# The first two feature tiles multiplied in parts of 256 tokens, with 256 columns normed first

## The chip, the cores and the metric

The kernel runs on one core of a Trainium2 chip. Its time is that of one execution on the device in microseconds (us); the figure for a kernel is the median of several executions. The engines are TensorE (PE in the profile, with PEld for its weight loads), ScalarE (ACT), VectorE (DVE), GpSimd (POOL) and SyncE (SP), which issues most DMAs.

## What is computed

One layer of a diffusion backbone over 1024 tokens of width 1024, with 256 context tokens. The part that matters here is the beginning: the adaLN modulation of the normed input, and the first column products with `w_in`.

```python
shift, scale, gate = adaln(c, w_ada, b_ada)          # silu(c) @ w_ada + b_ada
h = rmsnorm(x, norm_g) * (1 + scale[:, None]) + shift[:, None]
q, k, v, za, u, bg, cg, zc = jnp.split(h @ w_in, SPLIT_POINTS, axis=-1)
...
attn = neighbourhood_attention(q, k, heads(v), kc, vc, rpb) * jax.nn.silu(za)
conv = bg * centred_short_conv(cg * u, conv_w, conv_b) * jax.nn.silu(zc)
x_new = x + gate[:, None] * (jnp.concatenate([attn, conv], axis=-1) @ w_out)
```

## The kernel before

**Tiles.** The tokens come as eight tiles `xx[0]` to `xx[7]` of 128 tokens by 1024 features, four for each half of the sequence. Each is squared and summed on ACT (`square`, 607), its sum is turned into 1/rms by an addition on DVE and a power on POOL (`root`, 613), and DVE multiplies the tile by it in place (`norm`, 617). PE then transposes 128 features (one of eight feature tiles k) of four token tiles into one PSUM bank, a `tr` tile (`transposed`, 694). There are two buffers of `tr`; the modulation rows `mods[m]` (638) take one of them while they are summed. `turn` (700) applies scale and shift and splits the result into a high part `hh[k]` (ACT, type fp32r) and a low part `hl[k]`: a second copy in full precision, `hw`, is made by ACT or DVE, and DVE subtracts the high part from it (`modulated`, 673).

**Products.** `first_columns(half, k)` (719) multiplies three blocks of 128 columns of `w_in` (for u, the gate and c) by the 512 tokens of one half: high by high, low weights by high, high weights by low, nine matmuls into three PSUM banks `acc0`, which collect over all eight k. The weights come as chunks (`load_chunks`, 563); `split_chunk` (764) casts one on ACT and subtracts on DVE. `keep_clock` (586) issues matmuls on zeros that only keep TensorE busy.

**Modulation.** `w_ada` comes in slabs of 256 columns, two for each pair m of feature tiles (shift and scale, `load_slab`, 553). `products(m, j)` (638) multiplies the SiLU of the conditioning by slab (m, j): unsplit for (0, 0), (0, 1) and (1, 0); slab (1, 1) and later ones are split by `cast_slab` (620) and `rest_of` (628) into a high and a low part, with one pass for each. `row_copy` (649) takes the sums to SBUF on ACT (on DVE for m = 0), and `modulation` (655) transposes them and makes scale and shift `ab` on DVE for two feature tiles. So k = 2 and 3 can be turned only when slabs (1, 0) and (1, 1) have gone through.

**What sets the order.** In this section, `strict` (545) holds all engines and SP: every instruction of an engine is chained behind the one written before it (`ordered`, 44 to 60). The order of lines 767 to 834 is thus the order in which each engine works. SP issues loads in the written order (567 to 577, then at 812, 813, 818, 825, 826 and 832). Slabs after the first two share three buffers, so a later load waits until an earlier slab has been read.

Before, all four token tiles of the first half are normed whole and transposed for k = 0 and 1, both are turned and multiplied at 512 tokens, the second half is normed, and then come products(1, 0), the transposes of the second half, the split slab's products(1, 1), and only then `first_columns(1, 0)` (821).

Of the kernel before, what the change touches and what calls it, by code (L numbers as in the profile page):

```python
# [10 lines left out]
F32 = mybir.dt.float32  # L11
F32R = mybir.dt.float32r
BF16 = mybir.dt.bfloat16
AF = mybir.ActivationFunctionType
# [5 lines left out]
P = 128  # L20
# [19 lines left out]
def body(tc, es, x, ctxt, w_ada, b_ada, w_in, q_g, k_g, rpbr, w_out, vecs, cst, out):  # L40
# [522 lines left out]
    def load_chunks(ks):  # L563
        for k in ks:
            chunks[k] = chunk_load(CU, k)

    load_slab(0, 0)
    load_slab(0, 1)
    load_x(range(4))
    load_chunks([0])  # L570
    load_x([4, 5])
    load_chunks([1])
    load_x([6, 7])
    load_slab(1, 0)
    load_slab(1, 1)
# [31 lines left out]
    def square(xtile, n):  # L607

        sqj = cvp.tile([P, D], BF16, name="sqj", tag="cu", bufs=1)
        sums[n] = xp.tile([P, 1], F32, name="xss", tag="xss", bufs=4)  # L610
        act.activation(sqj, xtile, AF.Square, scale=1.0 / 32, accum_out=sums[n])

    def root(n):
        dve.tensor_scalar(sums[n], sums[n], EPS, None, ALU.add)
        pool.tensor_tensor(sums[n], sums[n], mhalf[:, 0:1], ALU.pow)

    def norm(xtile, n):
        dve.tensor_scalar(xtile, xtile, sums[n], None, ALU.mult)

    def cast_slab(m, j, part, cast):  # L620

# [33 lines left out]
    def modulation(m, rw):  # L655

        n, ks = 4 if m else 2, slice(2 * m, 2 * m + 2)
        pm = mods[m]
        for j in range(2):
            for i in range(2):  # L660
                pe.transpose(pm[:, n * (2 * j + i):n * (2 * j + i + 1)], rw[:, 256 * j + i * P:256 * j + (i + 1) * P],
                             ident[:n, :n])
        both = lambda v: v[:, ks].rearrange("p (k o) -> p k o", o=1).broadcast_to([P, 2, 2])
        abk = ab[:, ks].rearrange("p k (w j) -> p j k w", w=2)
        pm = pm[:, 0:4 * n].rearrange("p (j k w) -> p j k w", j=2, k=2)
        dve.tensor_tensor(abk[:, 0], pm[:, 0, :, 0:2], both(bsh), ALU.add)
        dve.tensor_tensor(abk[:, 1], pm[:, 1, :, 0:2], both(b1), ALU.add)
        if n > 2:
            for j in range(2):
                dve.tensor_tensor(abk[:, j], abk[:, j], pm[:, j, :, 2:4], ALU.add)  # L670
        dve.tensor_tensor(abk[:, 1], abk[:, 1], both(ng), ALU.mult)

    def modulated(hi, lo, ps, k, w, on, between=None):

        n = len(ps.shape) > 2 and 512 or 256
# [3 lines left out]
        if n == 512:  # L679
            hv = hv.rearrange("p (r b c) -> p r b c", r=8, b=4)  # L680
        act.activation(hi, ps, AF.Identity, bias=sh, scale=sc)
        if on is act:
            act.activation(hv, ps, AF.Identity, bias=sh, scale=sc)
        else:
            dve.tensor_scalar(hv, ps, sc, sh, ALU.mult, ALU.add)
        if between:
            between()
        dve.tensor_tensor(lo, hv, hi.bitcast(F32), ALU.subtract)

    def rows_of(v, half):  # L690

        return v.rearrange("p (b r c) -> p r b c", b=4, r=16)[:, 8 * half:8 * half + 8]
# [4 lines left out]
        for i in ts:  # L697
            pe.transpose(pts[half, k][:, i * P:(i + 1) * P], xx[4 * half + i][:, k * P:(k + 1) * P], ident)

    def turn(half, k, on, between=None):  # L700

        modulated(rows_of(hh[k], half), rows_of(hl[k], half),
                  pts.pop((half, k))[:].rearrange("p (r b c) -> p r b c", r=8, b=4), k, 0, on, between)

    def transposed_ctx(k2):
        pts[k2] = tr()
# [9 lines left out]
            k = 2 * k2 + kk  # L716
            modulated(hc[k // 4][:, k % 4, 0], hc[k // 4][:, k % 4, 1], pts[k2][:, kk * 256:(kk + 1) * 256], k, 1, (act, dve)[kk])

    def first_columns(half, k, part=range(3)):

        wh, wl = chunks[k][:2]
        h_, l_ = (v.rearrange("p (b r c) -> p b (r c)", b=4, r=16)[:, :, 128 * half:128 * half + 128]
                  for v in (hh[k], hl[k]))
        for i in part:
            for u in (0, 2, 1):
                uc = slice(u * P, (u + 1) * P)
                pe.matmul(acc0[u][half], (wl if i == 1 else wh)[:, uc], l_ if i == 2 else h_,
                          start=k == 0 and i == 0, stop=k == KT - 1 and i == 2)

    def gains_load():  # L730

# [32 lines left out]
    def split_chunk(k):  # L764
        chunks[k] = chunk_split(chunks[k])
# [2 lines left out]

    products(0, 0)
    products(0, 1)  # L770
    square(xx[0], 0)
    root(0)
    keep_clock(2)
    rw = row_copy(0)
    square(xx[1], 1)
    root(1)
    norm(xx[0], 0)
    square(xx[2], 2)
    root(2)
    modulation(0, rw)  # L780
    keep_clock(2)
    for t in range(1, 4):
        for k in range(2):
            transposed(0, k, [t - 1])
        keep_clock((5, 2, 3)[t - 1])
        norm(xx[t], t)
        if t == 1:
            square(xx[3], 3)
            root(3)
    for k in range(2):  # L790
        transposed(0, k, [3])
    split_chunk(0)
    square(xx[4], 4)
    root(4)
    turn(0, 0, dve)
    first_columns(0, 0)
    turn(0, 1, dve, lambda: split_chunk(1))
    for t in range(5, 8):
        square(xx[t], t)
        root(t)  # L800
        norm(xx[t - 1], t - 1)
    first_columns(0, 1)
    norm(xx[7], 7)
    cast_slab(1, 1, 0, act.copy)
    cast_slab(1, 1, 1, dve.tensor_copy)
    rest_of(1, 1, 0)
    rest_of(1, 1, 1)
    products(1, 0, range(6))
    transposed(1, 0)
    products(1, 0, range(6, KT))  # L810
    turn(1, 0, act)
    load_slab(2, 1)
    load_chunks([4, 5])
    products(1, 1, parts=(0,))
# [2 lines left out]
    products(1, 1, range(4, KT), (1,))  # L817
    load_slab(3, 0)
    split_chunk(2)
    turn(1, 1, act)  # L820
    first_columns(1, 0)
    rw = row_copy(1)
    split_chunk(3)
    split(2, 0, 0)
    load_slab(3, 1)
    load_chunks([6, 7])
    transposed(0, 2)
    modulation(1, rw)
# [720 lines left out]
```

## Time and profile before

| what | before |
|---|---|
| median of 3 runs | 631.23 us (630.48 to 631.58) |
| the profiled execution | 630.4 us |
| its span, first to last instruction | 628.6 us |
| mean granted TensorE clock | 0.999 |
| HBM traffic | read 89.04 MB, written 39.04 MB |

The times of single instructions below are from that profiled execution and count from the start of its span. A row of the timeline gives start, duration, engine, line, operation, what it writes and reads, shapes, and in brackets the engine's idle time before it with what ended it. Most instructions here have line 55, since the helper of the strict order emits them; they are told apart by the tiles they write. A row with x18 merges 18 instructions of a kind.

### The profile page before, as it was taken

The numbers are of one execution on the slowest core, as the hardware profiler recorded it, in microseconds if no ns is written. First come the engines' busy times: TensorE is split into PE (matmuls) and PEld (weight loads), VectorE is DVE, ScalarE is ACT, GpSimd is POOL, SyncE is SP. The second block draws the span as 40 slices with busy tenths as digits, with TensorE's granted clock in tenths as the row PEclk, the third lists the DMA queues.
The fourth block names the chain that finished last, engine by engine and source line by source line (L and its number), as shares of the span: only waits on it lengthen the run. The fifth ranks groups of instructions, "written<-read, shape, count | busy, mean of one in ns | idle before, by whom it ended". The sixth has DMA issues, their size and how long they took to land.

```text
span 628.6 us, 10005 instructions
## 1 busy us (share of the span) xinstructions
PE 621.7 (99%) x3487; PEld 538.5 (86%) x3488; DVE 433.5 (69%) x889; ACT 326.5 (52%) x712; POOL 77.6 (12%) x102
## 2 busy tenths in 40 slices
PE   8999999999999999999999999999999999999998
PEld 3577899999999999888888888888888888888887
DVE  1887858866866855568897879988998865594111
ACT  3777835524625545346576568566774845450000
POOL 1305014113223221100000000000000002004200
PEclk9999999999999999999999999999999999999999
DMA  8983737967784995885474553775542235963621
GB/s 316 347 282 124 178 111 259 286 204 244 236 293 137 302 320 181 298 264 214 144 238 140 192 172 127 214 254 181 190 136 76 61 93 163 357 226 121 213 102 50
DMA packets 104030, 126.45 MB, mean 201 GB/s; under 512 B 10689, under 2 KB 70553, under 8 KB 102700
## 3 DMA queue, kind: packets, MB, share of 16 engines
q1 hardware_dynamic: 97516, 114.24, 55.3%
q10 hardware_dynamic: 6208, 11.05, 5.6%
q0 software_dynamic: 256, 0.54, 0.3%
q8 instruction: 27, 0.44, 0.3%
q14 instruction: 23, 0.19, 0.1%
HBM read 89.04 MB, written 39.04 MB: 204 GB/s over the span
## 4 chain that ended last, share of the span: by engine, by line
PE 96%; DMA 2%; SPq 1%; ACT 0%; issue 0%; DVE 0%; ACTq 0%
PE pu L55 29%; PE pacc L55 21%; PE po L55 8%; PE acc L55 6%; PE pout L75 5%; PE pout L74 5%; PE pout L76 5%; PE tr L55 4%; PE cacc L55 4%; PE pss L55 3%; PE pc L55 2%; PE pmx L55 2%; DMA xx<-in_x 2%; PE trA L55 1%; PE trB L55 1%; SPq L55 1%
## 5 line engine op out<-in xcount | busy, mean ns | idle before, releaser
L55 PE MATMUL pu<-h,uh 128*128 128x512 f32 x544 | 170.0, 394 | 0.0
L55 PE MATMUL pacc<-w,h 128*128 128x384 f32 x768 | 138.4, 337 | 0.0
L55 PEld LDWEIGHTS pacc<-w,h 128*128 128x128 f32 x768 | 132.7, 188 | 0.2
L55 PEld LDWEIGHTS pu<-h,uh 128*128 128x128 f32 x544 | 97.6, 188 | 16.8 <-ACT zs L55 0.2
L55 PE MATMUL pu<-h,ul 128*128 128x512 f32 x272 | 106.6, 392 | 0.0
L55 PEld LDWEIGHTS pu<-h,ul 128*128 128x128 f32 x272 | 51.1, 188 | 11.2
L55 POOL TENSOR_TENSOR ss<-ss,few 128x4 f32<-128x4 f32 (+1 forms) x40 | 41.9, 1049 | 124.8 <-DVE ss L55 124.8
L75 PE MATMUL pout<-wol,yh 128*128 128x512 f32 (+2 forms) x136 | 51.6, 379 | 0.0
L74 PE MATMUL pout<-woh,yh 128*128 128x512 f32 (+2 forms) x136 | 51.5, 379 | 0.0
L76 PE MATMUL pout<-woh,yl 128*128 128x512 f32 (+2 forms) x136 | 50.8, 379 | 0.0
L55 PE MATMUL acc<-h,w 128*128 128x512 f32 x144 | 38.1, 404 | 0.8 <-ACT h L55 0.8
L55 ACT ACTIVATE sq<-pacc 128x256 f32<-128x256 f32 x32 | 12.4, 388 | 47.5 <-PE pacc L55 43.7
L55 DVE TENSOR_REDUCE rm<-pmx 128x2 f32<-128x256 f32 (+1 forms) x33 | 13.8, 417 | 32.7 <-PE pmx L55 32.6
L55 ACT COPY mg<-pmx 128x256 f32<-128x256 f32 (+1 forms) x33 | 12.1, 366 | 46.4 <-PE pmx L55 42.0
L55 DVE TENSOR_TENSOR mx<-mx,sb 128x372 f32<-128x372 f32 (+2 forms) x64 | 31.9, 498 | 1.9
L55 PE MATMUL po<-phl,v 128*65 128x276 f32 (+2 forms) x192 | 32.0, 269 | 0.0
L55 DVE TENSOR_REDUCE ss<-sq 128x4 f32<-128x260 f32 (+1 forms) x40 | 15.7, 392 | 23.6 <-ACT sq L55 23.6
L55 ACT ACTIVATE qn<-pacc,ss 128x64 f32<-128x64 f32 x128 | 30.2, 333 | 3.0 <-POOL ss L55 3.0
L55 PEld LDWEIGHTS acc<-h,w 128*128 128x128 f32 x144 | 25.5, 188 | 6.5 <-ACT h L55 1.2
L1479 DVE TENSOR_TENSOR ot<-pout,xr 128x512 f32<-128x512 f32 (+2 forms) x9 | 5.7, 632 | 35.4 <-PE pout L76 33.3
L55 ACT COPY sc<-pc 128x512 f32<-128x512 f32 x32 | 18.8, 589 | 21.1 <-PE pc L55 21.0
L74 PEld LDWEIGHTS pout<-woh,yh 128*128 128x128 f32 x136 | 25.6, 188 | 4.7
(159 smaller groups left out, 1194.4 us busy)
## 6 DMA issues: line engine op xcount, KB each, us to landing
uraw<-in_w_in SPq DMA_DIRECT2D x34, 256.0 KB
q_d<-qs SPq DMA_DIRECT2D x32, 256.0 KB
k_s<-k_d SPq DMA_DIRECT2D x8, 1024.0 KB
q_s<-q_d SPq DMA_DIRECT2D x16, 512.0 KB
wr<-in_w_in SPq DMA_DIRECT2D x40, 192.0 KB
slab<-in_w_ada SPq DMA_DIRECT2D x6, 1024.0 KB
v_d<-vs SPq DMA_DIRECT2D x20, 260.0 KB
v<-v_d SPq DMA_DIRECT2D x16, 325.0 KB
```

The lines of the kernel that those rows point to most:

```text
L55: i = emit(*a, **kw)
L74: i = pe.matmul(ps, ah, bh, start=first, stop=False)
L75: pe.matmul(ps, ah, bl, start=False, stop=False)
L76: pe.matmul(ps, al, bh, start=False, stop=last)
L1479: dve.tensor_tensor(ot[:, c], ps[c.start][:, c], xr[:, c], ALU.add)
```

## The change

The first half of the tokens is taken in two parts q of 256 tokens for k = 0 and 1: `turn` and `first_columns` get an argument q. Token tiles are first normed in columns 0 to 255 alone, which is all that k = 0 and 1 need; the other 768 columns follow later by `norm_rest`, on DVE for tiles 0, 1, 2, 6 and 7 and on ACT for tiles 3, 4 and 5. The loads of x and of the chunks change places, `root` and `norm` change places, `first_columns(1, 0)` stands ahead of the split slab's products, and `row_copy(1)` ahead of `turn(1, 1)`. The casts of slab (1, 1) swap engines. The matmuls of `keep_clock` among these lines go from 2 + 2 + 5 + 2 + 3 to 2 + 4.

```diff
-    load_x(range(4))
+    load_x([0, 1])
     load_chunks([0])
+    load_x([2, 3])
+    load_chunks([1])
     load_x([4, 5])
-    load_chunks([1])
     load_x([6, 7])
...
-        sums[n] = xp.tile([P, 1], F32, name="xss", tag="xss", bufs=4)
+        sums[n] = xp.tile([P, 1], F32, name="xss", tag="xss", bufs=8)
...
-    def norm(xtile, n):
-        dve.tensor_scalar(xtile, xtile, sums[n], None, ALU.mult)
+    def norm(xtile, n, cols=slice(0, D)):
+        dve.tensor_scalar(xtile[:, cols], xtile[:, cols], sums[n], None, ALU.mult)
+
+    def norm_rest(t, on):
+
+        v = xx[t][:, 256:]
+        if on is act:
+            act.activation(v, v, AF.Identity, scale=sums[t])
+        else:
+            dve.tensor_scalar(v, v, sums[t], None, ALU.mult)
...
-    def turn(half, k, on, between=None):
+    def turn(half, k, on, between=None, q=None):
 
-        modulated(rows_of(hh[k], half), rows_of(hl[k], half),
-                  pts.pop((half, k))[:].rearrange("p (r b c) -> p r b c", r=8, b=4), k, 0, on, between)
+        rows = slice(0, 8) if q is None else slice(4 * q, 4 * q + 4)
+        ps = pts[half, k] if q == 0 else pts.pop((half, k))
+        modulated(rows_of(hh[k], half)[:, rows], rows_of(hl[k], half)[:, rows],
+                  ps[:].rearrange("p (r b c) -> p r b c", r=8, b=4)[:, rows], k, 0, on, between)
...
-    def first_columns(half, k, part=range(3)):
+    def first_columns(half, k, part=range(3), q=None):
...
+        at = slice(0, 128) if q is None else slice(64 * q, 64 * q + 64)
...
-                pe.matmul(acc0[u][half], (wl if i == 1 else wh)[:, uc], l_ if i == 2 else h_,
-                          start=k == 0 and i == 0, stop=k == KT - 1 and i == 2)
+                pe.matmul(acc0[u][half][:].rearrange("p (b t) -> p b t", b=4)[:, :, at],
+                          (wl if i == 1 else wh)[:, uc], l_ if i == 2 else h_,
+                          start=k == 0 and i == 0 and not q, stop=k == KT - 1 and i == 2, skip_group_check=True)
...
     products(0, 0)
     products(0, 1)
+    low = slice(0, 256)
     square(xx[0], 0)
     root(0)
     keep_clock(2)
     rw = row_copy(0)
     square(xx[1], 1)
+    norm(xx[0], 0, low)
     root(1)
-    norm(xx[0], 0)
+    split_chunk(0)
+    modulation(0, rw)
+    for k in range(2):
+        transposed(0, k, [0])
+    keep_clock(4)
     square(xx[2], 2)
+    norm(xx[1], 1, low)
+    for k in range(2):
+        transposed(0, k, [1])
+    turn(0, 0, dve, q=0)
+    first_columns(0, 0, q=0)
+    square(xx[3], 3)
     root(2)
-    modulation(0, rw)
-    keep_clock(2)
-    for t in range(1, 4):
-        for k in range(2):
-            transposed(0, k, [t - 1])
-        keep_clock((5, 2, 3)[t - 1])
-        norm(xx[t], t)
-        if t == 1:
-            square(xx[3], 3)
-            root(3)
+    split_chunk(1)
+    turn(0, 1, dve, lambda: norm(xx[2], 2, low), q=0)
+    root(3)
+    for k in range(2):
+        transposed(0, k, [2])
+    first_columns(0, 1, q=0)
+    norm(xx[3], 3, low)
     for k in range(2):
         transposed(0, k, [3])
-    split_chunk(0)
     square(xx[4], 4)
+    turn(0, 0, dve, q=1)
     root(4)
-    turn(0, 0, dve)
-    first_columns(0, 0)
-    turn(0, 1, dve, lambda: split_chunk(1))
+    first_columns(0, 0, q=1)
+    turn(0, 1, dve, q=1)
     for t in range(5, 8):
         square(xx[t], t)
+        norm(xx[t - 1], t - 1, low)
+        norm_rest(t - 5, dve)
         root(t)
-        norm(xx[t - 1], t - 1)
-    first_columns(0, 1)
-    norm(xx[7], 7)
-    cast_slab(1, 1, 0, act.copy)
-    cast_slab(1, 1, 1, dve.tensor_copy)
+    first_columns(0, 1, q=1)
+    norm_rest(3, act)
+    norm(xx[7], 7, low)
+    products(1, 0, range(6))
+    cast_slab(1, 1, 0, dve.tensor_copy)
+    transposed(1, 0)
+    turn(1, 0, act)
+    cast_slab(1, 1, 1, act.copy)
     rest_of(1, 1, 0)
     rest_of(1, 1, 1)
-    products(1, 0, range(6))
-    transposed(1, 0)
     products(1, 0, range(6, KT))
-    turn(1, 0, act)
+    first_columns(1, 0)
     load_slab(2, 1)
     load_chunks([4, 5])
     products(1, 1, parts=(0,))
...
     products(1, 1, range(4, KT), (1,))
     load_slab(3, 0)
     split_chunk(2)
+    rw = row_copy(1)
     turn(1, 1, act)
-    first_columns(1, 0)
-    rw = row_copy(1)
     split_chunk(3)
+    for t in (6, 7):
+        norm_rest(t, dve)
     split(2, 0, 0)
...
     transposed(0, 2)
     modulation(1, rw)
     turn(0, 2, dve)
+    for t in (4, 5):
+        norm_rest(t, act)
     split(2, 0, 1)
```

More of the change, by code (lines that the diff above doesn't have):

```diff
@@ L673, in modulated @@
     def modulated(hi, lo, ps, k, w, on, between=None):
-        n = len(ps.shape) > 2 and 512 or 256
+        rows = ps.shape[1] if len(ps.shape) > 2 else 0
+        n = rows * GW or 256
         sh, sc = (ab[:, k, 2 * w + j:2 * w + j + 1] for j in range(2))
@@ L678, in modulated @@
         hv = hw[:, :n]
-        if n == 512:
-            hv = hv.rearrange("p (r b c) -> p r b c", r=8, b=4)
+        if rows:
+            hv = hv.rearrange("p (r b c) -> p r b c", r=rows, b=4)
         act.activation(hi, ps, AF.Identity, bias=sh, scale=sc)
@@ L717, in turn_ctx @@
             modulated(hc[k // 4][:, k % 4, 0], hc[k // 4][:, k % 4, 1], pts[k2][:, kk * 256:(kk + 1) * 256], k, 1, (act, dve)[kk])
-    def first_columns(half, k, part=range(3)):
+    def first_columns(half, k, part=range(3), q=None):
         wh, wl = chunks[k][:2]
-        h_, l_ = (v.rearrange("p (b r c) -> p b (r c)", b=4, r=16)[:, :, 128 * half:128 * half + 128]
+        at = slice(0, 128) if q is None else slice(64 * q, 64 * q + 64)
+        h_, l_ = (v.rearrange("p (b r c) -> p b (r c)", b=4, r=16)[:, :, 128 * half + at.start:128 * half + at.stop]
                   for v in (hh[k], hl[k]))
```

## The prediction

> **What bounds the kernel now.** I read the page first, its busy times (part 1) and the chain that ended last (part 4).
>
> ```profile
> PE 621.7 (99%) x3487; PEld 538.5 (86%) x3488; DVE 433.5 (69%) x889; ACT 326.5 (52%) x712; POOL 77.6 (12%) x102
> PE 96%; DMA 2%; SPq 1%; ACT 0%; issue 0%; DVE 0%; ACTq 0%
> ```
>
> TensorE is busy nearly always and ends the chain. Where it is not, the table by stretches tells (columns: length, then busy us of PE, PEld, DVE, ACT and POOL, granted clock, DMA share, GB/s).
>
> ```profile
> 13.70:20.86 7.16, 5.05 (x26) 2.42 (x27) 4.85 (x15) 5.86 (x12) 4.12 (x5) 1.00 1.04 400
> 20.86:38.00 17.14, 17.13 (x90) 11.44 (x91) 13.82 (x26) 11.66 (x19) 2.77 (x3) 1.00 1.00 336
> 38.00:78.00 40.00, 39.96 (x238) 31.51 (x237) 33.04 (x59) 31.41 (x53) 8.51 (x17) 1.00 0.55 164
> 78.00:620.00 542.00, 541.47 (x3051) 483.12 (x3050) 380.38 (x787) 273.13 (x625) 61.38 (x69) 1.00 0.61 197
> ```
>
> From 20.86 to 620 us PE idles 0.01 + 0.04 + 0.53 = 0.58 us. So whatever PE does later there, the kernel ends later, one for one; a gain can only come from the stretch before 20.86. The timeline shows what follows that stretch, and the limit of a gain.
>
> ```profile
> 12.59 1.06 ACT L55 ACTIVATE sqj<-xx 128x1024 bf16<-128x1024 f32 x1 [7.33 <-DMA xx<-in_x]
> 13.89 1.06 ACT L55 ACTIVATE sqj<-xx 128x1024 bf16<-128x1024 f32 x1 [0.16 <-DMA xx<-in_x]
> 20.86 4.58 PE L55 MATMUL acc<-h,w 128*128 128x512 f32 x18 [0.76 <-ACT h L55]
> 25.38 2.75 PE L55 MATMUL tr<-slab,c 128*4 128x256 f32 x12
> 27.90 1.06 ACT L55 CAST slabh<-slab 128x1024 fp32r<-128x1024 f32 x1 [2.61 <-DMA slab<-in_w_ada]
> 28.06 0.66 PE L55 MATMUL tr<-ci,xx 128*128 128x128 f32 x4
> 31.88 2.23 PE L55 MATMUL acc<-h,w 128*128 128x512 f32 x9
> 33.95 0.60 PE L55 MATMUL tr<-ci,xx 128*128 128x128 f32 x4
> 37.59 2.53 PE L55 MATMUL acc<-h,w 128*128 128x512 f32 x9
> ```
>
> The first 18 matmuls of the column products start at 20.86. At 25.38 follow products(1, 0), which need slab (1, 0). ACT waits for slab (1, 1) until 27.90. Tiles of x come 13.89 - 12.59 = 1.3 us apart; a slab is twice a tile, so slab (1, 0) is there about 2.6 us before (1, 1), at 25.2 to 25.3. In both orders PE takes products(1, 0) right after first_columns(0, 0) and (0, 1), and nothing is moved from behind that point to before it. So the changed kernel can gain 25.38 - 25.2 = 0.2 us at most. What remains is what it loses.
>
> **The change part by part.** I put the new order of each engine's instructions on a time line by hand, each starting when its engine is free and its inputs are there, with these durations (groups of one shape, 12 to 40 us; the number after the comma is the mean ns):
>
> ```profile
> L55 ACT ACTIVATE h<-tr,ab 128x512 fp32r<-128x512 f32 x6 | 4.5, 775 | 3.4 <-DVE ab L55 1.9 <-PE tr L55 1.6
> L55 ACT CAST slabh<-slab 128x1024 fp32r<-128x1024 f32 x4 | 4.2, 1046 | 2.6 <-DMA slab<-in_w_ada 2.6
> L55 ACT ACTIVATE hw<-tr,ab 128x512 f32<-128x512 f32 x3 | 2.3, 771 | 0.0
> L55 ACT CAST w<-wr 128x384 fp32r<-128x384 f32 x4 | 2.0, 502 | 0.0
> L55 ACT COPY rw<-tr 4x512 f32<-4x512 f32 x1 | 0.6, 560 | 0.0
> ```
>
> ```profile
> L55 DVE TENSOR_SCALAR xx<-xx,xss 128x1024 f32<-128x1024 f32 x8 | 6.0, 752 | 1.3 <-POOL xss L55 1.3
> L55 DVE TENSOR_TENSOR slabl<-slab,slabh 128x1024 fp32r<-128x1024 f32 x4 | 4.8, 1222 | 0.7 <-ACT slabh L55 0.7
> L55 DVE TENSOR_TENSOR h<-hw,h 128x512 fp32r<-128x512 f32 x5 | 3.4, 689 | 0.7 <-ACT hw L55 0.7
> L55 DVE TENSOR_SCALAR hw<-tr,ab 128x512 f32<-128x512 f32 x3 | 2.4, 808 | 1.6 <-ACT h L55 1.6
> L55 DVE TENSOR_TENSOR w<-wr,w 128x384 fp32r<-128x384 f32 x4 | 2.2, 553 | 0.2 <-ACT w L55 0.2
> L55 DVE TENSOR_SCALAR xss<-xss 128x1 f32<-128x1 f32 x8 | 1.2, 150 | 9.5 <-ACT sqj L55 9.4
> ```
>
> ```profile
> 14.07 0.57 POOL L55 TENSOR_TENSOR xss<-xss,few 128x1 f32<-128x1 f32 x1 [12.70 <-DVE xss L55]
> 16.76 0.30 PE L55 MATMUL tr<-ci,xx 128*128 128x128 f32 x1 [0.46 <-DVE ab L55]
> 16.90 1.24 PE L55 MATMUL acc<-warm 128*128 128x512 bf16 x5
> 17.81 1.01 POOL L55 TENSOR_TENSOR xss<-xss,few 128x1 f32<-128x1 f32 x1 [0.29 <-DVE xss L55]
> 20.03 1.45 ACT L55 ACTIVATE h<-tr,ab 128x512 fp32r<-128x512 f32 x2 [0.64 <-PE tr L55]
> 20.84 0.81 DVE L55 TENSOR_SCALAR hw<-tr,ab 128x512 f32<-128x512 f32 x1 [0.70 <-ACT h L55]
> 30.52 0.62 PE L55 MATMUL tr<-slabl,c 128*4 128x256 f32 x4
> ```
>
> Back-to-back instructions overlap a little (two h of 0.775 take 1.45), some 0.1 us; a wait between engines costs 0.04 to 0.12. DVE's hw waits for ACT's h though both only read the PSUM bank, so I let every access of one bank by different engines wait for the last. By the same arithmetic the old order gives 20.96, 25.48, 28.2 and 37.5 us for the rows at 20.86, 25.38, 28.06 and 37.59.
>
> The shapes that before does not have: **a turn of 256 tokens** costs ACT 0.56 (0.775 less 256 of the 0.85 ns a column between the two casts), DVE 0.54 and 0.42 (1.05 ns a column between the two subtractions); ends are half and all of the 512 rows. **A norm of 256 columns** lies between 0.15 and 0.75: 0.30 by the line through 1 and 1024 columns; of 768 on DVE 0.60. **768 columns on ACT** lie between 0.83 (a cast's line) and 0.99 (plus the 0.16 that h costs over a cast): 0.93. **A matmul of 256 columns** lies between 0.11 (the slabl row's pitch) and 0.23 (512 columns): 0.12. The power on POOL takes 0.57 with DVE idle and 1.0 beside a norm; in the new order DVE waits idle for it: 0.57.
>
> *To 25.98: products(1, 0).* The first half's norms now go x0, x1, and x1's sum of squares ends at 15.0 as before. The second transpose of x0 still waits for the modulation's ab (16.76 before), now behind chunk 0's subtraction: 16.4. Four warm matmuls, x1's transposes, and ACT's h give the first 9 half matmuls at 18.3, 2.6 us earlier than 20.86. But then one line runs through ACT and DVE: ACT squares x3 (18.15 to 19.30), casts chunk 1 (to 19.70), and makes h for k = 1 (to 20.16); DVE waits for the cast, subtracts (to 20.29), makes hw (20.75), and only then norms x2 (20.97), since this norm stands inside the turn. x3's root stands behind that turn: eps 21.23, power, norm at 22.1 to 22.4. Its transposes, ACT's h at 22.7, hw, l, and the same for k = 1 put the end of the 36 half matmuls at 25.9. Moving chunk 0 ahead of x2 (4 x 0.15 us of transfer) delays x2 by 0.5, which ACT's queue hides; from x6 on the loads come as before. **+0.6.**
>
> *To T10, the transposes of x4 to x7 (28.06 before).* Before, root(t) stood ahead of norm(t-1), so POOL's power ran beside a norm. Now norm(t-1) and norm_rest come first, then root(t): per tile 0.22 + 0.52 + 0.15 + 0.12 + 0.57 + 0.04 = 1.62 us in a line. Norm 4 starts at 25.2, norm 7 at 25.2 + 3 x 1.62 = 30.1, ends 30.4. PE has ended the 12 products at 28.6 and waits 1.8 us. T10 at 30.44: **+2.4 in all.** Behind it, 4 products (0.87), first_columns(1, 0) from 31.85 (its h is there at 31.8, its l at 33.2, just in time), then the split slab's 16 products and T11, all covered: 36.4 against 33.95 for the same work.
>
> *To T02, the transposes of x0 to x3 at 33.95.* They need a buffer of tr; there are two, mods[1] holds one, so turn(1, 1) must have read the other.
>
> ```profile
> 31.61 0.78 ACT L55 ACTIVATE h<-tr,ab 128x512 fp32r<-128x512 f32 x1 [0.92 <-PE tr L55]
> 36.76 0.78 ACT L55 ACTIVATE h<-tr,ab 128x512 fp32r<-128x512 f32 x1 [1.89 <-DVE ab L55]
> ```
>
> Before, first_columns(1, 0) (31.88, 2.23 us) hid that turn (31.61 to 33.1). Now it is gone from there, and row_copy(1) stands ahead of the turn on ACT and waits for the last product: 0.17 + 0.46 + 0.68 + 0.78 + 0.06 = 2.1 us of PE idle. T02 at 38.5, first_columns(1, 1) 39.3 to 41.4: **+4.6 in all.**
>
> *To T12, the transposes of x4 to x7 for k = 2.* They need columns 256 and up of x4 and x5, which ACT norms behind h of turn(0, 2). That h waited for ab before (1.89 us). Now DVE does ahead of ab: l from 38.5 (0.61), chunk 3 (0.47), two norm_rest (1.04), the slab's subtraction (1.14), ab (0.5): 42.3. ACT: h 0.68, two rests of 0.83 and 0.93: 44.7. PE idles from 41.4 for 3.3 us. T12 at 44.8 against 37.05 by the same arithmetic: **+7.7**. Behind it h and l of turn(0, 2) are there, which saves two waits of 0.1 each; slabs and chunks keep their lead. I end at **+7.4**.
>
> Slabs 2 and 3 are asked for up to 7 us later, since SP waits for buffers whose readers moved; their readers move as far.
>
> The profiled execution took 630.4 us (span 628.6): 637.8. The median of the three runs, 631.2, lies 0.8 above it: **638.6**. With each new shape at its low end the sum is +5.5, with the power at 1.0 +9.6.
>
> **The rivals.** *The clock drops.* The rows:
>
> ```profile
> 1.38 2.74 PE L55 MATMUL acc<-warm 128*128 128x512 bf16 x6 [1.38 <-POOL c L55]
> 620.00:625.80 5.80, 5.80 (x43) 5.66 (x41) 0.56 (x1) 0.00 (x0) 0.00 (x0) 1.00 0.21 79
> 626.00:628.60 2.60, 0.00 (x0) 0.00 (x0) 0.14 (x1) 0.00 (x0) 0.00 (x0) 0.71 0.09 25
> ```
>
> The first matmuls take 0.43 us a piece, later ones 0.22, and after PE's last one at 625.8 the clock falls within the last stretch. With the waits of 1.8, 2.1 and 3.3 us, and 6 warm matmuls after 13.7 us where the code had 14, it may fall once: some 4.5 us of work at half speed, as at the start, is +2.2: 640.8. The Trainium skill (TensorE: Matmul & The Clock Gate, HAM oscillation) allows idle gaps up to about 3.4 us, just over the longest I work out; by it the sum stays +7.4, and the trace's last stretch is less patient.
>
> *T12 does not wait.* If ACT is through with the rests in time, +7.4 - 3.2 = +4.2: 635.4. It speaks against it that ACT took h, casts and squares in written order throughout.
>
> *No slower.* If ACT and DVE took what is ready instead of the written order (turn(1, 1) ahead of row_copy(1), roots ahead of rests), all three waits would close; norm 7 would have to end by 28.5, 1.9 earlier than worked out, and PE would start products(1, 0) at 25.2: -0.2, 631.0. Every row of before in written order speaks against it.
>
> **How the numbers follow.** Forecast 0.60 (636.7 to 640.8 alone), the clock 0.25, no wait at T12 0.10, no slower 0.05. Range 635.4 to 641.4: it takes in the rival at T12 and the clock's, with the high end of the power left out in part. Over 0.2% (1.3 us, about what a measurement of this kernel can tell from no change): slower 0.95, same 0.04, faster 0.01.
>
> **What would show it.** PE's 9 half matmuls at about 18.3; products(1, 0) at 25.4 to 26.5; then PE idle ahead of tr<-ci,xx three times, released by DVE xx (near 30), ACT hw (near 38) and ACT xx (near 44); first_columns(0, 2) near 45. Wrong would be an end of these products before 25, no idle at T02, or a granted clock below 1 between 16 and 50 us.

## The result, and the profile after

| | before | changed |
|---|---|---|
| median | 630.53 us (629.99 to 631.58, 6 runs) | 639.95 us (637.57 to 643.32, 6 runs) |
| the profiled execution | 630.4 us, span 628.6 | 638.4 us, span 636.6 |
| mean granted clock in it | 0.999 | 0.997 |

The ratio is 1.0149, 95% interval 1.0118 to 1.0181: 9.4 us slower. Forecast were 638.6 us and a range of 635.4 to 641.4.

The page of the changed kernel, its first busy row and its chain:

```profile
PE 622.7 (98%) x3498; PEld 539.5 (85%) x3498; DVE 434.5 (68%) x898; ACT 329.6 (52%) x717; POOL 76.8 (12%) x102
PE 87%; DMA 4%; DVE 3%; ACT 3%; POOL 2%; issue 1%; ACTq 0%; DVEq 0%; POOLq 0%; SPq 0%
```

TensorE does hardly more work (622.7 against 621.7 us busy), yet the chain, 96% PE before, now runs through DMA, DVE, ACT and POOL for 12% of the span: it goes back past waits of PE. The table by stretches of the changed kernel says where (length, then busy us of PE, PEld, DVE, ACT, POOL, granted clock, DMA share, GB/s):

```profile
24.62:43.68 19.06, 14.21 (x71) 8.51 (x71) 11.79 (x26) 10.81 (x16) 1.65 (x3) 0.91 0.67 224
43.68:78.00 34.32, 33.19 (x202) 26.20 (x201) 26.25 (x44) 25.02 (x40) 8.44 (x12) 1.00 0.55 170
78.00:540.00 462.00, 461.50 (x2703) 416.56 (x2702) 350.59 (x743) 261.60 (x607) 52.52 (x66) 1.00 0.60 196
```

From products(1, 0) to first_columns(0, 2) PE idles 19.06 - 14.21 = 4.85 us, with the clock below 1; then 1.13 us more before 78; from there to 540 us, 0.50, as before. The timeline of PE in the changed kernel shows each wait (start, duration, what, and in brackets the idle time before it with its releaser):

```profile
16.80 1.66 PE L55 MATMUL acc<-h,w 128*128 128x256 f32 x9 [0.55 <-ACT h L55]
24.62 2.75 PE L55 MATMUL tr<-slab,c 128*4 128x256 f32 x12
29.07 0.33 PE L55 MATMUL tr<-ci,xx 128*128 128x128 f32 x1 [1.21 <-DVE xx L55]
29.32 1.03 PE L55 MATMUL tr<-slab,c 128*4 128x256 f32 x4
36.93 0.66 PE L55 MATMUL tr<-ci,xx 128*128 128x128 f32 x4 [2.00 <-ACT hw L55]
37.85 3.56 PE L55 MATMUL acc<-h,w 128*128 128x512 f32 x9
42.55 0.33 PE L55 MATMUL tr<-ci,xx 128*128 128x128 f32 x1 [1.14 <-ACT xx L55]
43.38 0.55 PE L55 MATMUL tr<-ci,xx 128*128 128x128 f32 x3 [0.50 <-ACT xx L55]
43.68 1.64 PE L55 MATMUL acc<-h,w 128*128 128x512 f32 x6
76.15 0.66 PE L55 MATMUL tr<-ci,xc 128*128 128x128 f32 x4 [1.13 <-ACT hw L55]
```

These starts can't be set beside those of before as they stand, for x arrived at another time. ACT squares x1 as soon as it has landed; in the changed kernel's timeline that row is

```profile
12.30 1.06 ACT L55 ACTIVATE sqj<-xx 128x1024 bf16<-128x1024 f32 x1 [0.17 <-DMA xx<-in_x]
```

against 13.89 before, though nothing ahead of x1 was changed. T10, T02 and T12 are the transposes that the forecast names so. T10 is read by the four products behind it, since the last of its four transposes is what waits now; PE's row of before for them is

```profile
28.65 1.03 PE L55 MATMUL tr<-slab,c 128*4 128x256 f32 x4
```

Taken from the start of x1's square, the steps of the forecast read:

| step | before | changed | later by | forecast |
|---|---|---|---|---|
| products(1, 0) | 11.49 | 12.32 | +0.83 | +0.6 |
| the products behind T10 | 14.76 | 17.02 | +2.26 | +2.4 |
| T02 | 20.06 | 24.63 | +4.57 | +4.6 |
| first_columns(0, 2) | 23.70 | 31.38 | +7.68 | +7.4 |
| end of the span | 614.7 | 624.3 | +9.6 | +7.4 |

The four steps came as forecast, within 0.3 us. Behind them another 1.9 us were lost in this execution that the forecast did not have.

### The profile page after: what moved, and what is told of

Same layout as the page of the kernel before. It is cut to its first block, busy times and chain, and to the rows that moved or that the text cites. A ratio compares the mean times of both kernels' runs of the same rounds, so it can differ in the third digit from the quotient of the medians.

```text
span 636.6 us, 10042 instructions
## 1 busy us (share of the span) xinstructions
PE 622.7 (98%) x3498; PEld 539.5 (85%) x3498; DVE 434.5 (68%) x898; ACT 329.6 (52%) x717; POOL 76.8 (12%) x102
## 4 chain that ended last, share of the span: by engine, by line
PE 87%; DMA 4%; DVE 3%; ACT 3%; POOL 2%; issue 1%; ACTq 0%; DVEq 0%; POOLq 0%; SPq 0%
PE pu L55 27%; PE pacc L55 21%; PE po L55 8%; PE pout L76 4%; PE pout L74 4%; PE pout L75 4%; PE cacc L55 3%; PE pss L55 3%; PE tr L55 3%; PE acc L55 3%; PE pc L55 2%; PE pmx L55 2%; DMA woraw<-in_w_out 2%; PE trA L55 1%; POOL rg L55 1%
## 5 line engine op out<-in xcount | busy, mean ns | idle before, releaser
L55 PE MATMUL acc<-h,w 128*128 128x512 f32 (+1 forms) x162 | 40.2, 389 | 1.2 <-ACT h L55 1.1
L55 DVE TENSOR_REDUCE rm<-pmx 128x2 f32<-128x256 f32 (+1 forms) x33 | 13.8, 417 | 32.9 <-PE pmx L55 32.8
L55 PEld LDWEIGHTS acc<-h,w 128*128 128x128 f32 x162 | 27.6, 193 | 6.8 <-ACT h L55 2.0
L76 PEld LDWEIGHTS pout<-woh,yl 128*128 128x128 f32 x136 | 25.6, 188 | 5.1 <-DVE yl L1482 0.4
```

The costliest lines, as they stand in the source:

```text
L55: i = emit(*a, **kw)
L76: pe.matmul(ps, al, bh, start=False, stop=last)
```

## The experiments

Two theories were set against each other, with a third beside them. **Three waits**: the time is lost where PE waits for ACT and DVE at T10, T02 and T12, each for an order that was changed. **The parts**: 36 half matmuls with more weight loads and small instructions cost it. **The clock**: the waits let the granted clock drop, and that costs it.

### e0_again: the changed kernel once more

> The changed kernel as it stands, for its spread beside the others on one chip. By the theory of the three waits (transposes of x4 to x7 behind norm 7, of x0 to x3 behind turn(1, 1), of x4 to x7 for k = 2 behind the rests) it lies 7 to 8 us over the kernel before in every run; by the clock rival the runs spread by over 3 us and those with a lower mean granted clock are the longer ones.

639.17 us (637.48 to 640.53), ratio 1.015 (1.0128 to 1.0172). The same waits stand in its trace, but the clock was at half for three times as long; the row of its table by stretches:

```profile
38.85:49.09 10.24, 8.66 (x26) 6.11 (x25) 7.70 (x13) 6.68 (x8) 0.00 (x0) 0.50 0.23 69
```

Its span is 638.8, 2.2 longer than the first trace's 636.6. So the clock makes two executions of this kernel differ by about that much. The four times spread over 3.05 us, and the longest is the one with the lowest mean granted clock (0.992), as the clock theory had it; what the clock does to the median is e5's question.

### e2_root: the power beside a norm again

```diff
     for t in range(5, 8):
         square(xx[t], t)
+        root(t)
         norm(xx[t - 1], t - 1, low)
         norm_rest(t - 5, dve)
-        root(t)
     first_columns(0, 1, q=1)
-    norm_rest(3, act)
     norm(xx[7], 7, low)
+    norm_rest(3, act)
```

> Only root(t) is put back ahead of norm(t-1) in the loop over tiles 5 to 7, and norm 7 ahead of norm_rest(3). Theory of the waits: POOL's power runs beside DVE's norms again, the 1.6 us of PE idle ahead of the second half's transposes near 29 us go, and the time falls by 1.6 to 2.0 us against the changed kernel. Rival, the cut into 256 tokens (36 half matmuls, twice the fixed costs of the turns) is what costs: no change, since nothing of that is touched. Rival, the clock: less idle, so a fall of up to 2 us more in runs that had a drop.

638.67 us (636.63 to 639.04), ratio 1.0137 (1.0117 to 1.0157). In PE's timeline the wait at T10 is gone, and the others stand:

```profile
37.06 0.65 PE L55 MATMUL tr<-ci,xx 128*128 128x128 f32 x4 [2.00 <-ACT hw L55]
42.68 0.33 PE L55 MATMUL tr<-ci,xx 128*128 128x128 f32 x1 [0.82 <-ACT xx L55]
```

x1's square starts at 14.02 there, so T02 is at 23.04 from it instead of 24.63: 1.6 us earlier, as the time line had it (0.15 of it ahead of products(1, 0), which start 12.16 us after x1's square there and 12.32 in the changed kernel). In the median only 0.5 us of the expected 1.6 to 2.0 is to be seen beside e0_again; the intervals overlap. The trace bears the step out, the time does not decide it.

### e3_rests: the late norms ahead of T12

```diff
-    norm_rest(3, act)
+    for t in (3, 4, 5):
+        norm_rest(t, act)
...
     split_chunk(2)
+    for t in (6, 7):
+        norm_rest(t, dve)
     rw = row_copy(1)
     turn(1, 1, act)
     split_chunk(3)
-    for t in (6, 7):
-        norm_rest(t, dve)
...
-    for t in (4, 5):
-        norm_rest(t, act)
```

> Only the rests of tiles 4 to 7 are moved: 4 and 5 on ACT right behind rest 3, where ACT idles from 26.6 to 29.4 us, and 6 and 7 on DVE ahead of row_copy(1), where DVE idles from 34.3 to 36.9 us. Theory of the waits: the transposes for k = 2 no longer wait for ACT, scale and shift come 1 us earlier, and the time falls by 2.5 us (1.6 by the wait in the profile, up to 2.9 at full clock). Rival of the 256-token cut: no change. Rival of the clock: the stretch from 38.6 to 42.0 us at half clock goes too.

635.89 us (635.6 to 636.97), ratio 1.0098 (1.0081 to 1.0115): 3.3 us less than e0_again, from moving four instructions. PE's timeline has the other two waits unchanged, and none at T12:

```profile
29.68 0.33 PE L55 MATMUL tr<-ci,xx 128*128 128x128 f32 x1 [1.20 <-DVE xx L55]
37.55 0.66 PE L55 MATMUL tr<-ci,xx 128*128 128x128 f32 x4 [2.00 <-ACT hw L55]
```

All the parts of 256 tokens are still in this kernel. The third wait is the largest term, as forecast (3.3 us). Three of these four executions have a granted clock of 1.000 and none of e0's has, so some of the 3.3 can be the clock's; by the table of steps T12 is worth 7.68 - 4.57 = 3.1.

### e5_zero: the waits filled with matmuls that add zeros

```diff
+    def keep_zero(n):
+
+        for _ in range(n):
+            pe.matmul(acc0[2][1], warm[:, :P], warm, start=False, stop=False, skip_group_check=True)
...
-    transposed(1, 0)
+    transposed(1, 0, range(3))
+    keep_clock(5)
+    transposed(1, 0, [3])
...
+    keep_zero(8)
     transposed(0, 2)
...
     first_columns(1, 1)
+    keep_zero(11)
     transposed(1, 2)
```

> The changed kernel with matmuls on zeros in the three waits: 5 ahead of the last of the second half's transposes, 8 ahead of the transposes of x0 to x3 for k = 2, 11 ahead of those of x4 to x7 for k = 2 (1.1, 1.7 and 2.4 us at full clock, each within its wait). Theory of the waits: PE has nothing else to do there, so the time stays at +7 us or falls by under 1.5 us. Rival, the clock is the cause: granted clock 0.999, no half clock near 40 us, and a fall of 2 us or more; in any case a smaller spread than the changed kernel's 5.8 us if the clock makes the spread.

638.88 us (637.14 to 639.15), ratio 1.0141 (1.0123 to 1.0159). The granted clock of the profiled execution is 1.000, and the median is 0.3 us less than e0_again. PE's timeline has

```profile
25.75 2.75 PE L55 MATMUL tr<-slab,c 128*4 128x256 f32 x12
44.79 2.33 PE L55 MATMUL acc<-h,w 128*128 128x512 f32 x9
```

From products(1, 0) to first_columns(0, 2) it takes 44.79 - 25.75 = 19.04 us at full clock, and 19.06 in the changed kernel's trace with its half clock: there the clock cost nothing. In other executions it does cost. Of the changed kernel's ten times (six and e0's four) the six with a mean granted clock of 0.996 or 0.997 lie between 637.5 and 639.9 us, the four with less between 640.0 and 643.3. The median of the six, 638.7, is 0.9 below that of the ten. So the clock widens the spread and owns about 1 us of the median, not the 9 that it lost. (This trace has no wait at the transposes of xc either, with 24 more matmuls ahead of them, so its median differs from e0's by more than the clock.)

### e7_second: the kernel before, with the new order of the second half alone

```diff
-    cast_slab(1, 1, 0, act.copy)
-    cast_slab(1, 1, 1, dve.tensor_copy)
-    rest_of(1, 1, 0)
-    rest_of(1, 1, 1)
     products(1, 0, range(6))
+    cast_slab(1, 1, 0, dve.tensor_copy)
     transposed(1, 0)
-    products(1, 0, range(6, KT))
     turn(1, 0, act)
+    cast_slab(1, 1, 1, act.copy)
+    rest_of(1, 1, 0)
+    rest_of(1, 1, 1)
+    products(1, 0, range(6, KT))
+    first_columns(1, 0)
...
-    turn(1, 1, act)
-    first_columns(1, 0)
     rw = row_copy(1)
+    turn(1, 1, act)
```

> The kernel before with only the changed order of the second half: first_columns(1, 0) ahead of the split slab's products, row_copy(1) ahead of turn(1, 1), the casts of slab (1, 1) on the other engines. No parts, no norm_rest. Theory of the three waits: one of them alone, at the transposes of x0 to x3 for k = 2, 2.05 us, released by ACT hw, and 0.4 us at first_columns(0, 2): 2.6 us above the kernel before, 632.2 to 633.2. It has as many instructions as the kernel before, so if the wait at the transposes of xc near 76 us hangs on where an instruction fetch falls, there is none here. Rival, the parts themselves: within 0.5 us of the kernel before.

632.83 us (632.28 to 633.21), before 630.18 beside it, ratio 1.0041 (1.0029 to 1.0054): 2.65 us, the amount expected, without a single part of 256 tokens. There is no wait at the transposes of xc, which was expected too. PE's timeline:

```profile
35.19 0.66 PE L55 MATMUL tr<-ci,xx 128*128 128x128 f32 x4 [2.00 <-ACT hw L55]
36.11 3.90 PE L55 MATMUL acc<-h,w 128*128 128x512 f32 x9
```

The wait is the changed kernel's to a hundredth. The nine matmuls behind it took 3.90 us where they take 2.53 or less at full speed; the stretch has half the clock:

```profile
36.08:39.49 3.41, 3.41 (x10) 2.72 (x10) 2.27 (x8) 1.52 (x3) 0.00 (x0) 0.50 0.34 119
```

So in this execution the clock that drops behind the wait does cost, since no second wait swallows it, and the 0.4 us expected at first_columns(0, 2) are not there. That the median came out as expected is in part luck: taken from x1's square (12.84), this execution ends 618.2 us on, 3.5 later than before's 614.7, 2.0 by the wait and 1.5 by the clock. The times do not show the clock's part: the one execution at 1.000 took 632.57 us, in the middle of the five.

### e6_first: the new first half with the old order of the second

```diff
+        root(t)
         norm(xx[t - 1], t - 1, low)
         norm_rest(t - 5, dve)
-        root(t)
...
-    norm_rest(3, act)
     norm(xx[7], 7, low)
+    norm_rest(3, act)
+    cast_slab(1, 1, 0, act.copy)
+    cast_slab(1, 1, 1, dve.tensor_copy)
+    rest_of(1, 1, 0)
+    rest_of(1, 1, 1)
     products(1, 0, range(6))
-    cast_slab(1, 1, 0, dve.tensor_copy)
     transposed(1, 0)
+    products(1, 0, range(6, KT))
     turn(1, 0, act)
-    cast_slab(1, 1, 1, act.copy)
-    rest_of(1, 1, 0)
-    rest_of(1, 1, 1)
-    products(1, 0, range(6, KT))
-    first_columns(1, 0)
+    for t in (4, 5):
+        norm_rest(t, act)
...
-    rw = row_copy(1)
+    for t in (6, 7):
+        norm_rest(t, dve)
     turn(1, 1, act)
+    first_columns(1, 0)
+    rw = row_copy(1)
     split_chunk(3)
-    for t in (6, 7):
-        norm_rest(t, dve)
...
-    for t in (4, 5):
-        norm_rest(t, act)
```

> The changed kernel's first half (parts of 256 tokens, 256 columns normed first, the loads) with the old order of the second half: the split slab's products ahead of first_columns(1, 0), turn(1, 1) ahead of row_copy(1), the casts of slab (1, 1) back on their engines, root(t) ahead of norm(t-1), and all norm_rest ahead of the transposes that need them. Theory of the three waits: none of them is left; by the same hand-made time line first_columns(0, 2) comes 1.0 us later than in the kernel before, of which 0.6 stood at products(1, 0) already: 630.0 to 631.5 where before gives 629.6 to 630.5, or up to 1.1 more if TensorE waits at the transposes of xc near 76 us as in the changed kernel. Rival, the parts themselves: 36 half matmuls with twice the weight loads and 40 small instructions on ACT and DVE cost what the change lost; then it stays at 635 or above.

632.89 us (631.78 to 633.81), ratio 1.0044 (1.0029 to 1.0058): 2.7 us above before. All three waits are gone, and the rival of the parts (635 or above) falls; but 2.7 is more than the 1.0, or 2.1 with the wait near 76 us, that were expected. PE's timeline has the wait at the transposes of xc (its waits from 24 to 80 us: 1.2 for ACT hw there, and 0.3) and a late start (the view behind the second row ends at 26 us, hence x3):

```profile
14.77 0.40 PE L55 MATMUL tr<-ci,rw 2*128 2x2 f32 x4 [0.24 <-DVE rw L55]
25.53 0.81 PE L55 MATMUL tr<-slab,c 128*4 128x256 f32 x3
38.27 2.53 PE L55 MATMUL acc<-h,w 128*128 128x512 f32 x9 [0.35 <-ACT h L55]
```

x1's square starts at 12.32, as in the changed kernel (12.30), but products(1, 0) come at 25.53 and not at 24.62. What is later by the same 0.91 us is the row of the first modulation's transposes, 14.77 against 13.86, and with it ab. Over all nine traces of this head, products(1, 0) start at the later of two times: 12.17 us after the start of x1's square, and 10.76 us after the modulation's transposes (largest miss 0.01 us):

| run | x1's square | modulation's transposes | later of the two | products(1, 0) |
|---|---|---|---|---|
| changed | 12.30 | 13.86 | 24.62 | 24.62 |
| e2_root | 14.02 | 15.09 | 26.19 | 26.18 |
| e3_rests | 13.07 | 13.75 | 25.24 | 25.25 |
| e6_first | 12.32 | 14.77 | 25.53 | 25.53 |
| e8_more | 12.90 | 15.04 | 25.80 | 25.81 |

In the old head, x1 alone decides: 11.49, 11.46, 11.55 and 11.47 us in the four traces (before, e7, e9, e10) in which the slab was there in time. So with x1 as early as here the new head is 13.21 - 11.49 = 1.7 us late; with 1.2 and 0.3 that makes 3.2 in this trace, where the medians differ by 2.7, since the head's share moves with x1.

### e1_row: row_copy(1) behind turn(1, 1)

```diff
-    rw = row_copy(1)
     turn(1, 1, act)
+    rw = row_copy(1)
```

> The changed kernel with row_copy(1) behind turn(1, 1) again, as before the change. Theory of the three waits: the wait at the transposes of x0 to x3 for k = 2 goes from 2.0 to 1.1 us (the turn's own two passes are left, since first_columns(1, 0) no longer covers them), and 0.2 of that is given back at T12: 0.7 us less than the changed kernel, 638.5 to 639.3 in the median. Rival, a clock that drops with the waits: as the three waits stay, the clock still drops, and nothing is gained that can be measured.

639.19 us (637.82 to 642.84), ratio 1.0155 (1.013 to 1.0179): not to be told from the changed kernel. In its trace the wait at T02 went from 2.00 to 1.07, as expected, and T12's became

```profile
41.78 0.48 PE L55 MATMUL tr<-ci,xx 128*128 128x128 f32 x1 [2.62 <-DVE hw L55]
43.16 3.04 PE L55 MATMUL acc<-h,w 128*128 128x512 f32 x8
```

so first_columns(0, 2) starts at 43.16 instead of 43.68, but at half clock. Inconclusive in the time: what the row gains is less than what the clock scatters.

### e4_all: all three, with first_columns(1, 0) left where the change put it

The edits of e1, e2 and e3 together, norm_rest(6) and (7) ahead of turn(1, 1).

> The changed kernel with root(t) ahead of norm(t-1), all norm_rest ahead of the transposes that need them, and row_copy(1) behind turn(1, 1); first_columns(1, 0) stays ahead of the split slab's products. Theory of the three waits: the waits at T10 and T12 are gone, 1.1 us are left at T02 and 0.4 at first_columns(0, 2); 2.7 us above the kernel before on the time line, 632.3 to 634.0 with the wait near 76 us. Rival, effects that add up only in part (a clock that drops all the same, transfers that come later): 635 or above, no better than the rests alone.

634.31 us (633.33 to 635.26), ratio 1.0067 (1.0053 to 1.0082). PE's timeline has what was expected up to first_columns(0, 2):

```profile
34.76 0.66 PE L55 MATMUL tr<-ci,xx 128*128 128x128 f32 x4 [1.07 <-ACT hw L55]
38.26 0.63 PE L55 MATMUL tr<-ci,xx 128*128 128x128 f32 x4 [0.24 <-DVE ab L55]
39.23 2.53 PE L55 MATMUL acc<-h,w 128*128 128x512 f32 x9 [0.35 <-ACT h L55]
```

With 1.14 us at xc these are 2.8; the head, by the two times above (12.21 and 13.95), is 1.04 late: 3.8 of the 4.1 us measured. The expected 634.0 fell short for the head, as in e6.

### The wait at the transposes of xc: e8, e9, e10, e11

What PE waits for near 76 us begins with a chunk of w_q. ACT casts four of them in a row, then makes h and hw that free the buffer for these transposes. Before, ACT's timeline has the four at once:

```profile
65.30 2.23 ACT L55 CAST w<-wr 128x384 fp32r<-128x384 f32 x4 [0.39 <-DMA wr<-in_w_in]
```

In the changed kernel the fourth comes late:

```profile
71.21 1.68 ACT L55 CAST w<-wr 128x384 fp32r<-128x384 f32 x3 [0.43 <-DMA wr<-in_w_in]
74.23 0.51 ACT L55 CAST w<-wr 128x384 fp32r<-128x384 f32 x1 [1.34 <-DMA wr<-in_w_in]
```

The trace has a queue of its own for instructions, with transfers of 16 KB, some 0.9 us long. The DMA view of the changed kernel from 70 to 72.5 us has one (packets, MB, share):

```profile
q8 instruction: 1, 0.02, 2.3%
```

A load tells of its landing in 16 parts, as many as the core has DMA engines, and behind such a transfer one part of the next loads lands 1.0 to 1.8 us after the others. The transfers come after some 120 matmuls each by the trace's records, the third between PE's 339th and 345th in eleven of the fourteen traces (321st, 327th and 351st in the others). In the changed kernel it starts at 71.85 us, 1.2 us after the first of the five landings at that place; 15 parts of the fourth chunk are there at 72.92, the last at 74.21, and ACT casts at 74.23. In the kernel before it starts 2.45 us after the first landing, at 67.17, when the fourth chunk is there (66.98). The change put 10 more matmuls ahead of it. If this is the cause, matmuls that do nothing must make the wait come and go, whatever the order.

```diff
+    def keep_small(n):
+
+        for _ in range(n):
+            pe.matmul(acc0[2][1][:, :64], warm[:, :P], warm[:, :64], start=True, stop=True)
...
     turn(0, 0, dve)
+    keep_small(8)
     first_columns(0, 0)
```

That is e9_eight, on the kernel before; e10_fourteen and e11_twenty have 14 and 20. In e8_more, e6_first gets 5 ahead of first_columns(0, 0, q=0), 12 ahead of the transposes of x2 and 5 ahead of first_columns(0, 0, q=1).

> e6_first with 22 small matmuls on zeros (64 columns, bf16) in three of TensorE's waits of the first half, which nothing reads. Theory of the instruction fetch: the third 16 KB transfer on the instruction queue comes at TensorE's 340th matmul in nine profiles; 17 matmuls ahead of the transposes of xc it makes a chunk of w_q land late and TensorE waits 1.0 to 1.2 us there (seven profiles), 9 ahead or 59 ahead it does not (three). Here it falls some 39 ahead: no wait at the transposes of xc, 1.1 us less than e6_first, 631.3 to 632.2 where before gives 630.2. Rival, the wait belongs to the changed order (chunks asked for later): it stays, and the time is that of e6_first, 632.9. Theory of the head: products(1, 0) start at the later of 12.26 us after x1 has landed and 10.76 us after the first modulation's transposes, as in eight profiles of this head; a rival that takes x1 alone, as the prediction did, has them at 12.4.

632.20 us (630.86 to 633.93, 12 runs), ratio 1.0031 (1.0017 to 1.0046). The wait is gone; PE's timeline has

```profile
69.94 0.60 PE L55 MATMUL tr<-ci,xc 128*128 128x128 f32 x4
```

and products(1, 0) come at 25.81, where the two times of the head give 25.80 and x1 alone 12.90 + 12.17 = 25.07. The fetch fell 54 matmuls ahead of xc, where some 39 were expected. The median is at the high end of what was expected, 0.7 us under e6_first; in this trace PE waits 1.35 us for yh at 556 us, where before has no wait.

> The kernel before with 8 small matmuls on zeros (64 columns, bf16) in the 0.76 us in which TensorE waits ahead of first_columns(0, 0), which nothing reads; nothing else is changed. Theory of the instruction fetch: it now falls 17 matmuls ahead of the transposes of xc, as in the changed kernel, and TensorE waits 1.0 to 1.2 us there: 631.0 to 631.5 where before gives 630.2, though no order was changed. Rival, the wait belongs to the changed order: no wait there, within 0.3 us of before. Theory of the head: products(1, 0) 11.56 us after x1 has landed, as in both profiles of the old head.

631.16 us (629.21 to 632.74, 12 runs), ratio 1.0013 (0.9999 to 1.0028). The expectation missed its own condition: the fetch came 12 matmuls ahead of xc, not 17, and 1.9 us after the first landing. There is no wait at xc in the trace. The median lies 1.2 us above before's all the same: the first six times lie between 629.21 and 630.86, as before, and the last six between 631.46 and 632.74. Whether those have the wait is not known.

> The kernel before with 14 small matmuls on zeros ahead of first_columns(0, 0) in place of the 8 of e9_eight. With those 8 the third instruction fetch came only 12 matmuls ahead of the transposes of xc and 1.9 us after the first of the landings there, later than the 17 matmuls and 1.2 to 1.3 us that were expected, and TensorE did not wait. Theory of the instruction fetch: with 14 it comes some 17 ahead, 1.1 to 1.4 us after that landing, and TensorE waits 1.0 to 1.2 us at the transposes of xc, with the order of the kernel before unchanged; 631.0 to 631.6 where before gives 630.0. Rival, the wait belongs to the changed order: no wait there, within 0.3 us of before.

631.62 us (631.08 to 633.53, 12 runs), ratio 1.0019 (1.0005 to 1.0033). The fetch starts 17 matmuls ahead, 1.25 us after the first landing, and the wait is there, in the order of the kernel before; PE, then ACT:

```profile
70.29 0.66 PE L55 MATMUL tr<-ci,xc 128*128 128x128 f32 x4 [1.17 <-ACT hw L55]
```

```profile
66.56 0.51 ACT L55 CAST w<-wr 128x384 fp32r<-128x384 f32 x1 [0.20 <-DMA wr<-in_w_in]
68.38 0.51 ACT L55 CAST w<-wr 128x384 fp32r<-128x384 f32 x1 [1.31 <-DMA wr<-in_w_in]
```

> The same with 20. Theory of the instruction fetch: some 22 matmuls ahead, 0.4 to 0.8 us after the first landing; the late landing is then an earlier chunk's, and TensorE still waits at the transposes of xc, 0.5 to 1.2 us, since ACT casts the four chunks in a row. Rival, the wait belongs to the changed order: no wait there, within 0.3 us of before.

631.31 us (630.76 to 632.92, 11 runs), ratio 1.0018 (1.0007 to 1.0028). The fetch starts 1.1 us after the first landing, and now the third of the four chunks is late; PE waits 1.14 us. And the first fetch, moved to 22.1 us, met slab (1, 0), which landed at 24.58; PE's row for products(1, 0) is

```profile
24.72 2.75 PE L55 MATMUL tr<-slab,c 128*4 128x256 f32 x12 [0.75 <-POOL xss L55]
```

The releaser named there had long been done. This is the bound that the forecast put on any gain (products(1, 0) not before their slab), seen in a trace: 0.14 us after the landing.

So 14 matmuls of nothing, placed where PE was idle, made the kernel before wait 1.17 us and cost it 1.6 in the medians (0.3 to 2.1 by the interval). The medians alone would not tell, since e9's is 1.2 up without the wait in its trace; the traces do. With the old order e10 and e11 have the wait, with the new order of either half e8 and e7 have none: it goes with where an instruction fetch falls, not with the changed order. No experiment pointed to an order that beats the kernel before: with the three waits and the one at xc gone, e8 is still 2.2 us above it.

## Why the prediction was right, and where it was not

**Bound and sign.** Right. PE was busy after 20.86 us, and the three waits put there are found again in the steps of the table, within 0.4 us each. The gain ended at the slab: e11 shows that bound directly.

**The durations** worked out for shapes that before did not have; the groups of the changed kernel's trace (behind the bar: busy us, mean ns of one):

```profile
L55 DVE TENSOR_SCALAR xx<-xx,xss 128x768 f32<-128x768 f32 x5 | 3.0, 615 | 0.0
L55 DVE TENSOR_SCALAR xx<-xx,xss 128x256 f32<-128x256 f32 x8 | 2.8, 349 | 2.8 <-POOL xss L55 2.7
L55 ACT ACTIVATE xx<-xx,xss 128x768 f32<-128x768 f32 x3 | 2.7, 924 | 0.0
L55 DVE TENSOR_SCALAR hw<-tr,ab 128x256 f32<-128x256 f32 x4 | 2.2, 541 | 2.4 <-ACT h L55 2.4
L55 ACT ACTIVATE h<-tr,ab 128x256 fp32r<-128x256 f32 x4 | 2.2, 563 | 2.5 <-PE tr L55 2.5
```

0.60, 0.30, 0.93, 0.54 and 0.56 were forecast. Only the norm of 256 columns was off, by 0.05.

**Products(1, 0), +0.6.** The one line through ACT and DVE that was worked out is there: with x1 as late as in the profile of before, the rule of the two times gives 13.89 + 12.17 = 26.06, where 25.98 was forecast. What failed is that a time worked out for one landing of x1 was carried to all executions. The new head has a second line, through the modulation, whose start doesn't move with x1. When x1 comes early, the old head gains all of it and the new one does not: +0.83 in the changed kernel's trace, +1.7 in e6's.

**T10, +2.4.** Right, by its mechanism; the number sets the last of the four transposes (30.44) against the first of before (28.06), and what PE lost by the products behind them is 2.26. The row shown for the power at 0.57 us (14.07) has DVE busy with the copy of rw beside it; the one with DVE idle is POOL's at 20.28, 0.55 us, and the value holds. DVE's timeline repeats every 27.05 - 25.44 = 1.61 us, where 1.62 was forecast, each time after a wait for POOL:

```profile
25.44 0.88 DVE L55 TENSOR_SCALAR xx<-xx,xss 128x256 f32<-128x256 f32 x2 [0.67 <-POOL xss L55]
27.05 0.88 DVE L55 TENSOR_SCALAR xx<-xx,xss 128x256 f32<-128x256 f32 x2 [0.66 <-POOL xss L55]
```

e2 takes this wait alone away.

**T02, 2.1 us.** Right: 2.00, and alone in e7. Of it 0.9 are the row copy and 1.1 the uncovered turn (e1 and e4: 1.07).

**T12, 3.3 us.** Right. The idle time before it is 1.64 us in the trace, but the nine matmuls ahead of it took 3.56 us at half clock: they filled a wait that would have been there anyway (1.64 and the 1.33 that they took beyond 2.23 make 3.0; e5, at full clock, is as long from products(1, 0) to first_columns(0, 2)). ACT's timeline is the line of the forecast:

```profile
40.90 0.78 ACT L55 ACTIVATE h<-tr,ab 128x512 fp32r<-128x512 f32 x1 [2.67 <-DVE ab L55]
41.57 1.75 ACT L55 ACTIVATE xx<-xx,xss 128x768 f32<-128x768 f32 x2
```

The rival that T12 does not wait falls with it; e3 is what it would have looked like.

**"I end at +7.4".** Here the sum was too small: it took for granted that nothing is late behind first_columns(0, 2). The wait at xc added 1.1 us, shown by e8, e10 and e11 to come from the number of matmuls ahead of an instruction fetch. Another 0.84 us were lost in the pout matmuls from 544 us on (89.42 us from the first to PE's last, 88.58 before), 0.27 of them in a wait for yh. That loss does not follow the change: e1, the changed kernel but for one row, takes 88.58 us there, and e9, the kernel before with 8 idle matmuls, 89.45; e2, e5 and e8 wait 0.8, 0.8 and 1.35 us for yh. Its cause stays open. In the medians the kernel lost 9.4 us where the sum says 7.4; that 638.6 still came within 1.4 us of 639.95 is in part luck, since it stands on a median of three, 631.23, that lay 0.7 us above the median of six.

**The clock.** The rival's event came, and its price of 2.2 us only in some executions: in the changed kernel's trace the clock was at half from 38.63 to 42.04, inside T12's wait, and cost nothing (e5). It costs where no wait covers it (e7's trace, and the longer one of e0); the four of ten executions with the lower clock took 2.3 us more in the median than the other six. The forecast counted it as a case of its own; it is better read as a part of the scatter, about 1 us of the median.

**No slower.** Falls: ACT and DVE kept the written order wherever a wait was read.

## What to carry to other kernels

When an order is changed, follow each engine's own line of instructions to the next thing that PE needs: four small instructions placed one PE wait too late cost some 3 us here, while the extra matmuls and instructions of the parts showed no cost beyond the later head. Work out a start from every input that it waits for, and ask which of them moves from run to run; the one that doesn't bind in the profile at hand may bind in the next. A change of a few instructions can move an instruction fetch onto a load that was just in time, so before a microsecond is put down to an order, try the old order with as many idle instructions.

## What the runs showed of the hardware

- The last of the 16 parts of a tile of x landed 0.35 to 2.2 us behind the middle one near 12 us, differently in each execution; ACT's square starts only when that one is there. x1's square started between 12.20 and 14.02 us in 14 traces.
- An instruction fetch of 16 KB has the same effect on the loads behind it, 1.0 to 1.8 us near the transposes of xc. The third came near PE's 340th matmul in eleven of 14 traces, at any time from 66.0 to 74.5 us.
- A wait of 2.00 us by itself was followed, 0.9 us after its end, by 3.41 us at half clock (e7); one of 1.07 us was not (e4). The Trainium skill (TensorE: Matmul & The Clock Gate, HAM oscillation) allows idle gaps up to about 3.4 us; these traces are less patient, since the clock fell after stretches of 3.41 us in which PE idled 1.6 to 2.6 us.
- The first modulation's transposes started at 13.8 to 15.2 us, the later the later the clock went to full speed at the beginning (4.1 to 7.1 us). It is the matmuls ahead of products(0, 0) that run at half clock: products(0, 0) themselves start behind that moment in all 14 traces (before: full clock from 5.88, products from 6.70).
